# Attention of block 1: values stationary, probabilities moving, and the gate applied to the transposed output

## The chip, the cores and the metric

The kernel runs on one core of a Trainium2 chip. The metric is device time in microseconds (us) of one execution of the whole program, median of several runs. TensorE (PE) multiplies matrices and does the transposes; VectorE (DVE), ScalarE (ACT) and GpSimd (POOL) work on tiles; SyncE (SP) issues most DMAs. In the rows, PEld is the loading of the stationary operand, which runs beside PE.

## The reference

Everything is float32; `x` is (1, 256, 2048): 256 tokens. The program is two layers of a gated convolution beside windowed attention (block 1), then an RWKV and a latent-attention mixer with a feed-forward part (block 2, which the change does not touch). What matters of block 1, in one layer:

```python
u = hn @ w_in[i]
a_val, a_glu, a_z, q, k, v, b_z = jnp.split(u, offs, axis=-1)
ya = _conformer_conv(a_val, a_glu, ...) * jax.nn.silu(a_z)
# attention: 16 query heads of 64, in 4 groups with one key and value head each
s = q·k * 64**-0.5 + bias_band            # window of 128 on both sides
m = maximum(max(s), sink);  e = exp(s - m)
denom = sum(e) + exp(sink - m)
yb = ((e / denom) @ v) * jax.nn.silu(b_z)
h = h + concatenate([ya, yb]) @ w_out[i]
```

With 256 tokens and blocks of 128 every query sees both blocks of keys, so a head's probabilities are a 256x256 matrix with the band in the bias.

## The kernel before, in words

**Projections.** The hidden state lies in memory with channels on the 128 partitions and 256 tokens along the free axis. A projection to 256 columns (`lin`) splits weights and activations into a high and a low half and adds three matmuls (L302, L303, L304) for each of 16 slices of channels and each of two output tiles: 96 matmuls. Weights come by DMA as `wraw`, in blocks of four slices (24 matmuls); ACT casts the high half (`whi`, L264) and DVE subtracts for the low half (`wlo`, L265), with three buffers of each. The sum stands in one of three PSUM buffers "lin".

**A layer.** `layer1` first projects the convolution's eight inputs, then keys and values, then goes through four attention steps j = 0 to 3. A step projects q (tile `q`, L478) and the gate `gz` = silu(b_z) with tokens on partitions (L490), calls `attend1` for four heads, and then has the 31 convolution steps of two channel tiles on ACT and DVE (`cy`, L501), which need nothing of the attention. Behind the loop follow the sum over channels (`cs`, L507), the four `z` projections, whose result DVE takes out of PSUM (L408), and `w_out`, attention half first.

**attend1 before.** For each of the four heads g: scores by four matmuls (L588), then bias, sink and maximum in one DVE reduction for each half (L593), into a tile of the ring "s", which has four buffers and also serves the `z` tiles. Then the sink's term `ex` (L596, L598), eight exponentials on ACT with their sums (L601), the sum and its reciprocal `den` on DVE (L603, L604). For each head four PE transposes of the probabilities into `ptr` (L611), a copy to `pT` on ACT (L613), and four matmuls `po` (L616) in which a 128x128 piece of `pT` is stationary and 64 columns of values `vd` move: the output has tokens on partitions. It is scaled by `den` (L619), multiplied by `gz` (L621), transposed by four PE transposes `pot` (L625) and split into `Y` (L626).

**Buffers and order.** The tiles `q`, `pT` and the outputs of the convolution come from rings with few buffers: tag "q" has two, tag "pT" two. In PSUM `ptr`, `pot` share two buffers, `sc` has two and `po` one. Each engine works through its instructions in a fixed order, made when the program is built: a scheduler merges the strands (attention, projections, weight loads and splits, convolution) by their readiness in its own model and by priorities, and within one engine nothing overtakes. PE fills the gaps of the attention with projection matmuls in this way.

Of the kernel before, what the change touches and what calls it, by code (L numbers as in the profile page):

```python
# [8 lines left out]
F32 = mybir.dt.float32  # L9
# [3 lines left out]
ALU = mybir.AluOpType  # L13
# [5 lines left out]
SEQ = 256  # L19
# [78 lines left out]
class Kern:  # L98
# [475 lines left out]
    def attend1(self, i, j, q, vd, gz, Y):  # L574
        nc = self.nc
        sk = self.sink[i][:, 4 * j : 4 * j + 4]
        mx = self.wk.tile([128, 4, 2], F32, tag="mx", name=self.nm("mx"))
        den = self.wk.tile([128, 4, 2], F32, tag="den", name=self.nm("den"))
        ex = self.wk.tile([128, 4, 2], F32, tag="ex", name=self.nm("ex"))
        s4 = []  # L580
        for g in range(4):
            h = 4 * j + g
            bt = self.wk.tile([128, 384], F32, tag="bt", name=self.nm("bt"))
            nc.gpsimd.dma_start(bt[:], self.bias_src(h))
            ps = self.psum("sc", [128, 2, SEQ], "sc")
            for qb in range(2):
                for u in range(2):
                    nc.tensor.matmul(ps[:, qb, :], lhsT=q[:, g, qb * 128 : qb * 128 + 128], rhs=self.ks[u][:, j, :],  # L588
                                     start=(u == 0), stop=(u == 1))
            s = self.wk.tile([128, 2, SEQ], F32, tag="s", bufs=4, name=self.nm("s"))  # L590
            for qb in range(2):
                o = 128 * (1 - qb)
                nc.vector.tensor_tensor_reduce(s[:, qb, :], ps[:, qb, :], bt[:, o : o + SEQ], 1.0, sk[:, g : g + 1],  # L593
                                               ALU.add, ALU.max, mx[:, g, qb : qb + 1])
            s4.append(s)
        nc.vector.tensor_tensor(ex[:], sk.unsqueeze(2).to_broadcast([128, 4, 2]), mx[:], ALU.subtract)  # L596
        nc.vector.tensor_scalar(mx[:], mx[:], -1.0, None, ALU.mult)
        nc.scalar.activation(ex[:], ex[:], AF.Exp)  # L598
        for g in range(4):
            for qb in range(2):  # L600
                nc.scalar.activation(s4[g][:, qb, :], s4[g][:, qb, :], AF.Exp, bias=mx[:, g, qb : qb + 1],  # L601
                                     accum_out=den[:, g, qb : qb + 1])
        nc.vector.tensor_tensor(den[:], den[:], ex[:], ALU.add)  # L603
        nc.vector.reciprocal(den[:], den[:])  # L604
        po = self.psum("o", [128, 2, 4, 64], "po")
        for g in range(4):
            s = s4[g]
            pt = self.psum("tr", [128, 2, SEQ], "ptr")
            for kb in range(2):
                for qb in range(2):  # L610
                    nc.tensor.transpose(pt[:, kb, qb * 128 : qb * 128 + 128], s[:, qb, kb * 128 : kb * 128 + 128], self.ident)  # L611
            pT = self.wk.tile([128, 2, SEQ], F32, tag="pT", name=self.nm("pT"))
            nc.scalar.copy(pT[:], pt[:])  # L613
            for qb in range(2):
                for kb in range(2):
                    nc.tensor.matmul(po[:, qb, g, :], lhsT=pT[:, kb, qb * 128 : qb * 128 + 128], rhs=vd[:, kb, j, :],  # L616
                                     start=(kb == 0), stop=(kb == 1))
        on = self.wk.tile([128, 2, 4, 64], F32, tag="pT", name=self.nm("on"))
        nc.vector.tensor_tensor(on[:], po[:], den[:].rearrange("p g b -> p b g").unsqueeze(3).to_broadcast([128, 2, 4, 64]), ALU.mult)  # L619
        on_ = on[:].rearrange("p b g c -> p b (g c)")  # L620
        nc.vector.tensor_tensor(on_, on_, gz[:], ALU.mult)  # L621
        pt = self.psum("tr", [128, 2, SEQ], "pot")
        for t in range(2):
            for qb in range(2):
                nc.tensor.transpose(pt[:, t, qb * 128 : qb * 128 + 128],  # L625
                                    on[:, qb, 2 * t : 2 * t + 2, :].rearrange("p g c -> p (g c)"), self.ident)  # L626
        self.split_pair(Y, 8 + 2 * j, pt[:])

    def embed_new(self, i):

# [851 lines left out]
```

## Time and profile before

| | |
|---|---|
| time, median of 3 runs | 2235.72 us (2234.7 to 2237.15) |
| profiled execution | 2232.6 us |
| its span, first to last instruction | 2230.7 us |
| PE busy | 2203.2 us, 99% |
| DVE busy | 1638.7 us, 73% |
| ACT busy | 1157.5 us, 52% |
| attention steps of layer 0 / layer 1 | about 140 to 290 us / 730 to 870 us |

Busy time is time in which an engine has at least one instruction running. Matmuls overlap in PE's pipeline, so that one of them lasts 0.28 us while the next starts 0.12 us later; what a matmul costs is read from start to start. An fp32 matmul is recorded as several passes, and the count behind the x counts passes.

### The profile page before, as it was taken

Reading aid. Unit: us, or ns where it says so; the run is one execution under the profiler, and the core shown is the slowest. Engines: PE = TensorE matmul, PEld = TensorE weight load, DVE = VectorE, ACT = ScalarE, POOL = GpSimd, SP = SyncE. Lnnn points to the kernel's source line nnn. Section 1 sums busy time; section 2 is a strip of 40 time slices with the busy share of each in tenths; the row PEclk is TensorE's granted clock in tenths of the full one; section 3 lists DMA queues with packets and bytes.
Section 4 is the critical chain, followed back from the end, with each engine's and each line's share of the span. In section 5 each row is a group of like instructions: output and inputs, shape, how many; then the busy total and the mean of one; then the engine's idle time right before and its main releaser. Section 6 shows DMA issues by size and latency. Waiting matters only on the chain.

```text
span 2230.7 us, 43513 instructions
## 1 busy us (share of the span) xinstructions
PE 2203.2 (99%) x17563; PEld 2134.6 (96%) x17563; DVE 1638.7 (73%) x2884; ACT 1157.5 (52%) x1694; POOL 106.6 (5%) x253
## 2 busy tenths in 40 slices
PE   8999999999999999999999999999999999999998
PEld 8999999999999999999999889999998999899987
DVE  6999988677999887677878886676665566556665
ACT  6456646454467555556656665355443444434443
POOL 3100000000000000002100000010000000000000
PEclk9999999999999999999999999999999999999999
DMA  7875557666665466667675434477655666556654
GB/s 239 241 208 158 158 180 214 187 204 183 184 185 161 143 196 212 212 202 230 197 189 142 130 118 136 147 233 226 182 188 191 187 183 187 189 189 185 184 189 142
DMA packets 382745, 413.23 MB, mean 185 GB/s; under 512 B 40472, under 2 KB 343829, under 8 KB 382160
## 3 DMA queue, kind: packets, MB, share of 16 engines
q1 hardware_dynamic: 344672, 366.06, 53.4%
q0 software_dynamic: 10960, 31.79, 4.5%
q10 hardware_dynamic: 26912, 12.60, 2.5%
q8 instruction: 138, 2.26, 0.4%
q14 instruction: 63, 0.52, 0.1%
HBM read 390.47 MB, written 19.92 MB: 184 GB/s over the span
## 4 chain that ended last, share of the span: by engine, by line
PE 96%; DVE 2%; ACT 1%; issue 0%; DMA 0%; ACTq 0%; SPq 0%; DVEq 0%
PE lin L302 25%; PE lin L304 25%; PE lin L303 25%; PE lin L1299 2%; PE lin L1300 2%; PE lin L1298 2%; PE dn L1300 2%; PE dn L1299 2%; PE dn L1298 2%; PE po L616 1%; PE sc L588 1%; PE lin L1136 1%; PE lin L1134 1%; PE lin L1135 1%; PE ptr L611 1%; PE pch L1017 1%
## 5 line engine op out<-in xcount | busy, mean ns | idle before, releaser
L264 ACT CAST whi<-wraw 128x1024 fp32r<-128x1024 f32 (+1 forms) x709 | 725.4, 1024 | 914.5 <-PE lin L303 632.4
L302 PE MATMUL lin<-xh,whi 128*128 128x256 f32 x4080 | 1158.8, 284 | 2.3 <-ACT ev L656 1.2
L304 PE MATMUL lin<-xh,wlo 128*128 128x256 f32 x4080 | 1157.7, 284 | 0.6 <-DVE wlo L265 0.6
L303 PE MATMUL lin<-xl,whi 128*128 128x256 f32 x4080 | 1157.4, 284 | 0.0
L265 DVE TENSOR_TENSOR wlo<-wraw,whi 128x1024 fp32r<-128x1024 f32 (+1 forms) x709 | 844.5, 1192 | 408.1 <-ACT whi L264 404.8
L302 PEld LDWEIGHTS lin<-xh,whi 128*128 128x128 f32 x4080 | 782.7, 192 | 5.5 <-issue 1.9
L304 PEld LDWEIGHTS lin<-xh,wlo 128*128 128x128 f32 x4080 | 782.7, 192 | 2.2 <-issue 1.0
L303 PEld LDWEIGHTS lin<-xl,whi 128*128 128x128 f32 x4080 | 782.7, 192 | 1.4 <-issue 1.0
L501 DVE SCALAR_TENSOR_TENSOR cy<-apad,vc_cw,cy 128x256 f32<-128x256 f32 x480 | 229.9, 481 | 7.8
L304 PE MATMUL lin<-whi,xl 128*128 128x256 f32 x320 | 91.7, 287 | 0.0
L302 PE MATMUL lin<-whi,xh 128*128 128x256 f32 x320 | 91.6, 286 | 0.0
L303 PE MATMUL lin<-wlo,xh 128*128 128x256 f32 x320 | 90.8, 284 | 0.0
L304 PE MATMUL lin<-yh,wlo 128*128 128x256 f32 x256 | 73.4, 288 | 0.8 <-DVE wlo L265 0.7
L302 PE MATMUL lin<-yh,whi 128*128 128x256 f32 x256 | 73.0, 286 | 0.2 <-ACT mla L1208 0.2
L303 PE MATMUL lin<-yl,whi 128*128 128x256 f32 x256 | 73.1, 286 | 0.0
L1299 PE MATMUL lin<-wlo,xh 128*128 128x512 f32 (+1 forms) x176 | 67.1, 381 | 0.5 <-DVE wlo L265 0.5
L1298 PE MATMUL lin<-whi,xh 128*128 128x512 f32 (+1 forms) x176 | 67.1, 381 | 0.4 <-ACT whi L264 0.4
L1298 PE MATMUL dn<-whi,xh 128*128 128x512 f32 (+1 forms) x176 | 67.0, 381 | 0.0
L1299 PE MATMUL dn<-wlo,xh 128*128 128x512 f32 (+1 forms) x176 | 67.0, 381 | 0.0
L1300 PE MATMUL lin<-whi,xl 128*128 128x512 f32 (+1 forms) x176 | 67.0, 381 | 0.0
L1300 PE MATMUL dn<-whi,xl 128*128 128x512 f32 (+1 forms) x176 | 67.0, 381 | 0.0
L302 PEld LDWEIGHTS lin<-whi,xh 128*128 128x128 f32 x320 | 61.3, 192 | 0.0
(533 smaller groups left out, 2505.5 us busy)
## 6 DMA issues: line engine op xcount, KB each, us to landing
wraw<-in_w_in_dram SPq DMA_DIRECT2D x244, 512.0 KB, 3.8
wraw<-in_w_out_dram SPq DMA_DIRECT2D x88, 512.0 KB, 3.8
wraw<-in_ffn_w_gate_dram SPq DMA_DIRECT2D x88, 512.0 KB, 3.6
wraw<-in_ffn_w_up_dram SPq DMA_DIRECT2D x88, 512.0 KB, 3.5
wraw<-in_ffn_w_down_dram SPq DMA_DIRECT2D x87, 512.0 KB, 3.7
wraw<-in_w_pg_dram SPq DMA_DIRECT2D x64, 512.0 KB, 4.5
bt<-btab POOLq DMA_DIRECT2D x32, 192.0 KB, 3.3
btab<-bF ACTq DMA_DIRECT2D x4, 1024.0 KB, 7.9
```

The costliest lines, as they stand in the source:

```text
L264: nc.scalar.copy(hi[:], src)
L265: self.lo = nc.vector.tensor_tensor(lo[:], src, hi[:].bitcast(F32), ALU.subtract)
L302: nc.tensor.matmul(ps[:, t, :], lhsT=h, rhs=xh_, start=((t, k) == first), stop=False)
L303: nc.tensor.matmul(ps[:, t, :], lhsT=h, rhs=xl_, start=False, stop=False)
L304: nc.tensor.matmul(ps[:, t, :], lhsT=l, rhs=xh_, start=False, stop=((t, k) == last))
L501: prev, tail = tail, nc.vector.scalar_tensor_tensor(y, ap[:, t, k : k + SEQ], cw[:, k : k + 1], y, ALU.mult, ALU.add)
L588: nc.tensor.matmul(ps[:, qb, :], lhsT=q[:, g, qb * 128 : qb * 128 + 128], rhs=self.ks[u][:, j, :], start=(u == 0), stop=(u == 1))
L611: nc.tensor.transpose(pt[:, kb, qb * 128 : qb * 128 + 128], s[:, qb, kb * 128 : kb * 128 + 128], self.ident)
L616: nc.tensor.matmul(po[:, qb, g, :], lhsT=pT[:, kb, qb * 128 : qb * 128 + 128], rhs=vd[:, kb, j, :], start=(kb == 0), stop=(kb == 1))
L1298: nc.tensor.matmul(ps, lhsT=zh, rhs=hi, start=(k == 0), stop=False)
L1299: nc.tensor.matmul(ps, lhsT=zh, rhs=lo, start=False, stop=False)
L1300: nc.tensor.matmul(ps, lhsT=zl, rhs=hi, start=False, stop=(k == nt - 1))
```

## The change

The product with the values is turned round. The values (64 columns) are stationary and 256 columns of `pT` move, so the output comes out with channels on partitions, as `Y` needs it: head 2t on partitions 0 to 63, head 2t+1 on partitions 64 to 127 of one tile. The gate and the softmax sum, which lie with tokens on partitions, are multiplied first (`gn`), transposed in place of the output (`pgt`, four transposes) and copied to `gT` by ACT; the output `y` is `po` times `gT`. `gT` and `y` take buffers of the tag "q".

```diff
@@ -602,29 +602,37 @@
                                      accum_out=den[:, g, qb : qb + 1])
         nc.vector.tensor_tensor(den[:], den[:], ex[:], ALU.add)
         nc.vector.reciprocal(den[:], den[:])
-        po = self.psum("o", [128, 2, 4, 64], "po")
-        for g in range(4):
-            s = s4[g]
-            pt = self.psum("tr", [128, 2, SEQ], "ptr")
-            for kb in range(2):
-                for qb in range(2):
-                    nc.tensor.transpose(pt[:, kb, qb * 128 : qb * 128 + 128], s[:, qb, kb * 128 : kb * 128 + 128], self.ident)
-            pT = self.wk.tile([128, 2, SEQ], F32, tag="pT", name=self.nm("pT"))
-            nc.scalar.copy(pT[:], pt[:])
-            for qb in range(2):
-                for kb in range(2):
-                    nc.tensor.matmul(po[:, qb, g, :], lhsT=pT[:, kb, qb * 128 : qb * 128 + 128], rhs=vd[:, kb, j, :],
-                                     start=(kb == 0), stop=(kb == 1))
-        on = self.wk.tile([128, 2, 4, 64], F32, tag="pT", name=self.nm("on"))
-        nc.vector.tensor_tensor(on[:], po[:], den[:].rearrange("p g b -> p b g").unsqueeze(3).to_broadcast([128, 2, 4, 64]), ALU.mult)
-        on_ = on[:].rearrange("p b g c -> p b (g c)")
-        nc.vector.tensor_tensor(on_, on_, gz[:], ALU.mult)
-        pt = self.psum("tr", [128, 2, SEQ], "pot")
+
+        gn = self.wk.tile([128, 2, 4, 64], F32, tag="pT", name=self.nm("gn"))
+        nc.vector.tensor_tensor(gn[:], gz[:].rearrange("p b (g c) -> p b g c", g=4),
+                                den[:].rearrange("p g b -> p b g").unsqueeze(3).to_broadcast([128, 2, 4, 64]), ALU.mult)
+        pt = self.psum("tr", [128, 2, SEQ], "pgt")
         for t in range(2):
             for qb in range(2):
                 nc.tensor.transpose(pt[:, t, qb * 128 : qb * 128 + 128],
-                                    on[:, qb, 2 * t : 2 * t + 2, :].rearrange("p g c -> p (g c)"), self.ident)
-        self.split_pair(Y, 8 + 2 * j, pt[:])
+                                    gn[:, qb, 2 * t : 2 * t + 2, :].rearrange("p g c -> p (g c)"), self.ident)
+        gT = self.wk.tile([128, 2, SEQ], F32, tag="q", name=self.nm("gT"))
+        nc.scalar.copy(gT[:], pt[:])
+
+        po = self.psum("o", [128, 2, SEQ], "po")
+        for t in range(2):
+            pTs = []
+            for h in range(2):
+                s = s4[2 * t + h]
+                pt = self.psum("tr", [128, 2, SEQ], "ptr")
+                for kb in range(2):
+                    for qb in range(2):
+                        nc.tensor.transpose(pt[:, kb, qb * 128 : qb * 128 + 128], s[:, qb, kb * 128 : kb * 128 + 128], self.ident)
+                pT = self.wk.tile([128, 2, SEQ], F32, tag="pT", name=self.nm("pT"))
+                nc.scalar.copy(pT[:], pt[:])
+                pTs.append(pT)
+            for kb in range(2):
+                for h in range(2):
+                    nc.tensor.matmul(po[64 * h : 64 * h + 64, t, :], lhsT=vd[:, kb, j, :], rhs=pTs[h][:, kb, :],
+                                     start=(t == 0 and kb == 0), stop=(t == 1 and kb == 1))
+        y = self.wk.tile([128, 2, SEQ], F32, tag="q", name=self.nm("ya"))
+        nc.vector.tensor_tensor(y[:], po[:], gT[:], ALU.mult)
+        self.split_pair(Y, 8 + 2 * j, y[:])
 
     def embed_new(self, i):
 
```

The order on PE in the last step (j = 3) of layer 0. `sc` are the last scores, `ptr` the transposes of the probabilities, `lin` with `xh`, `xl` projections. Before, from the first transposes of the step:

```order
L302 MATMUL lin_3450<-xh_88,whi_3459 128x256
L611 MATMUL ptr_3153<-cblk,s_3106 128x128
L303 MATMUL lin_3450<-xl_90,whi_3459 128x256
L304 MATMUL lin_3450<-xh_88,wlo_3460 128x256
L302 MATMUL lin_3450<-xh_88,whi_3459 128x256
L611 MATMUL ptr_3153<-cblk,s_3106 128x128 x3
```

The same place now:

```order
L588 MATMUL sc_3116<-kh,qs_2950 128x256
L588 MATMUL sc_3116<-kl,qs_2950 128x256
L303 MATMUL lin_3560<-xl_91,whi_3653 128x256
L304 MATMUL lin_3560<-xh_89,wlo_3654 128x256
L612 MATMUL pgt_3139<-cblk,gn_3137 128x128 x4
L625 MATMUL ptr_3147<-cblk,s_3091 128x128 x4
L625 MATMUL ptr_3154<-cblk,s_3101 128x128 x4
L631 MATMUL po_3146<-pT_3152,vd_1542 64x256
L625 MATMUL ptr_3165<-cblk,s_3111 128x128 x4
L302 MATMUL lin_3690<-xh_88,whi_3699 128x256
```

Before, the first transposes stand among the matmuls of a projection; now two projection matmuls stand between the last scores and the transposes of the gate, and those stand ahead of every transpose of the probabilities.

The order on DVE in the same step, around the softmax sum `den`; `cy` are convolution steps, `z` takes a `z` projection out of PSUM. Before:

```order
L501 SCALAR_TENSOR_TENSOR cy_261<-apad_1282,vc_cw_643,cy_261 128x256 x2
L408 TENSOR_TENSOR z_3441<-lin_3320,r_224 128x512
L501 SCALAR_TENSOR_TENSOR cy_261<-apad_1282,vc_cw_643,cy_261 128x256
L603 TENSOR_TENSOR den_3097<-den_3097,ex_3098 128x8
L501 SCALAR_TENSOR_TENSOR cy_261<-apad_1282,vc_cw_643,cy_261 128x256
L604 RECIPROCAL den_3097<-den_3097 128x8
L265 TENSOR_TENSOR wlo_3516<-wraw_3455,whi_3515 128x1024
```

And now:

```order
L501 SCALAR_TENSOR_TENSOR cy_261<-apad_1282,vc_cw_643,cy_261 128x256 x8
L603 TENSOR_TENSOR den_3082<-den_3082,ex_3083 128x8
L501 SCALAR_TENSOR_TENSOR cy_261<-apad_1282,vc_cw_643,cy_261 128x256
L604 RECIPROCAL den_3082<-den_3082 128x8
L501 SCALAR_TENSOR_TENSOR cy_261<-apad_1282,vc_cw_643,cy_261 128x256
L607 TENSOR_TENSOR gn_3137<-gz_3078,den_3082 128x512
L501 SCALAR_TENSOR_TENSOR cy_261<-apad_1282,vc_cw_643,cy_261 128x256 x5
L408 TENSOR_TENSOR z_3421<-lin_3300,r_224 128x512
```

The gate's product `gn` follows the reciprocal with one convolution step between, and the first `z` comes behind it instead of ahead of the sum.

The order on PE in step j = 2 of layer 1, the last three heads' values matmuls; `ppt` is a transpose of the embedding's part. Before, the last head:

```order
L303 MATMUL lin_8896<-wlo_8990,xh_5103 128x256
L304 MATMUL lin_8896<-whi_8989,xl_5105 128x256
L616 MATMUL po_8637<-vd_7466,pT_8665 128x64 x4
L616 MATMUL po_8637<-vd_7466,pT_8676 128x64 x4
L302 MATMUL lin_8896<-whi_8989,xh_5103 128x256
```

And now:

```order
L631 MATMUL po_8616<-pT_8622,vd_7446 64x256
L625 MATMUL ptr_8635<-cblk,s_8581 128x128 x4
L631 MATMUL po_8616<-pT_8629,vd_7446 64x256
L631 MATMUL po_8616<-pT_8622,vd_7446 64x256
L631 MATMUL po_8616<-pT_8629,vd_7446 64x256
L625 MATMUL ptr_8642<-cblk,s_8591 128x128 x4
L631 MATMUL po_8616<-pT_8640,vd_7446 64x256
L645 MATMUL ppt_8659<-cblk,pr_8657 128x128 x4
L631 MATMUL po_8616<-pT_8647,vd_7446 64x256
L631 MATMUL po_8616<-pT_8640,vd_7446 64x256
L631 MATMUL po_8616<-pT_8647,vd_7446 64x256
L302 MATMUL lin_9464<-xh_5082,whi_9473 128x256
```

Each pair of heads has one values matmul alone and then three together; before, the last run stands within a projection, now the next projection starts behind it.

## Rows read from the trace of the kernel before

**Rows 1.** The page: busy time of each engine with its share of the span, and the chain of work that ended last by engine.

```profile
PE 2203.2 (99%) x17563; PEld 2134.6 (96%) x17563; DVE 1638.7 (73%) x2884; ACT 1157.5 (52%) x1694; POOL 106.6 (5%) x253
...
PE 96%; DVE 2%; ACT 1%; issue 0%; DMA 0%; ACTq 0%; SPq 0%; DVEq 0%
```

**Rows 2.** The list of PE's waits, its first rows: what waited, for what, us in total, times, longest.

```profile
PE vps L170 <- DMA cblk<-in_c_blk_dram: 2.9, 1, 2.9
PE xt L356 <- DMA xr<-in_x_dram: 2.7, 1, 2.7
```

**Rows 3.** The timeline of PE at a values matmul of layer 0: start and duration in us, what.

```profile
175.23 0.28 PE L303 MATMUL lin<-wlo,xh 128*128 128x256 f32 x1
175.35 1.00 PE L616 MATMUL po<-vd,pT 128*128 128x64 f32 x8
...
176.37 0.28 PE L302 MATMUL lin<-whi,xh 128*128 128x256 f32 x1
```

**Rows 4.** The timeline of PE at the sum over channels, fp32 over 256 columns, and at the transposes of the output behind it.

```profile
275.89 2.32 PE L507 MATMUL cs<-cy,cblk 128*128 128x256 f32 x10
278.05 0.60 PE L625 MATMUL pot<-cblk,on 128*128 128x128 f32 x4
278.49 0.60 PE L507 MATMUL cs<-cy,cblk 128*128 128x256 f32 x2
```

**Rows 5.** The timeline of PE in block 2: a run of matmuls of which `pch` use 64 columns of the array and `po` 64 rows and 64 columns, between projection matmuls (rows and columns used stand behind the names, as 128\*64).

```profile
1183.83 0.28 PE L303 MATMUL lin<-xl,whi 128*128 128x256 f32 x1
1184.03 0.68 PE L1030 MATMUL pch<-big 128*64 128x64 f32 x8
1184.64 0.67 PE L1033 MATMUL po<-big,tx 64*64 64x64 f32 x8
...
1185.47 0.28 PE L302 MATMUL lin<-xh,whi 128*128 128x256 f32 x1
```

**Rows 6.** The timeline of PE in block 2: a run on 64 rows of the array, between projection matmuls.

```profile
1102.17 0.28 PE L302 MATMUL lin<-xh,whi 128*128 128x256 f32 x1
1102.38 1.13 PE L848 MATMUL pw<-hwz,la 64*128 64x256 f32 x4
...
1103.66 0.28 PE L304 MATMUL lin<-xh,wlo 128*128 128x256 f32 x1
```

**Rows 7.** The timeline of PE in block 2: two such matmuls of four passes each, `pw` on one half of the array's rows and `pa` on the other; the first pair and the last of four.

```profile
1023.23 0.48 PE L848 MATMUL pw<-hwz,la 64*128 64x256 f32 x1
1023.24 0.48 PE L854 MATMUL pa<-hwz,la 64*128 64x256 f32 x1
...
1023.99 0.38 PE L854 MATMUL pa<-hwz,la 64*128 64x256 f32 x1
```

**Rows 8.** Two answers on single lines. L408 (DVE takes `z` out of PSUM): what its idle time before it ended with, us and times. L584 (the bias row's load by POOL's queue): time from issue to landing.

```profile
  PE ptr L611: 1.6, 2
...
DMA to landing us min/median/max: 2.6/3.3/6.0
```

**Rows 9.** The timelines of PE, DVE and ACT in the last step of layer 0, from the last scores to the reciprocal of the softmax sum; in square brackets the idle time before and what ended it.

```profile
252.44 0.28 PE L588 MATMUL sc<-kl,qs 128*128 128x256 f32 x1
...
253.34 0.48 DVE L593 CUSTOM_DVE_ANT_0 s<-sc,bt,sink 128x256 f32<-128x256 f32 x1
...
254.15 0.48 DVE L501 SCALAR_TENSOR_TENSOR cy<-apad,vc_cw,cy 128x256 f32<-128x256 f32 x1
...
256.16 0.16 DVE L597 TENSOR_SCALAR mx<-mx 128x8 f32<-128x8 f32 x1
...
261.30 0.69 DVE L408 TENSOR_TENSOR z<-lin,r 128x512 f32<-128x512 f32 x1 [0.93 <-PE ptr L611]
...
262.78 0.17 DVE L603 TENSOR_TENSOR den<-den,ex 128x8 f32<-128x8 f32 x1 [0.40 <-ACT s L601]
...
263.26 0.20 DVE L604 RECIPROCAL den<-den 128x8 f32<-128x8 f32 x1
...
256.23 1.05 ACT L264 CAST whi<-wraw 128x1024 fp32r<-128x1024 f32 x1 [1.83 <-DVE cy L501]
...
258.59 0.21 ACT L598 ACTIVATE ex<-ex 128x8 f32<-128x8 f32 x1
258.71 0.49 ACT L601 ACTIVATE s<-s,mx 128x256 f32<-128x256 f32 x1
```

**Rows 10.** Groups by line: line, engine, operation, shape, passes or instructions | busy us, mean ns of one | idle time of the engine just before, and what ended it.

```profile
L611 PE MATMUL ptr<-cblk,s 128*128 128x128 f32 x128 | 21.2, 273 | 0.0
...
L613 ACT COPY pT<-ptr 128x512 f32<-128x512 f32 x32 | 17.7, 584 | 6.3 <-PE ptr L611 6.2
```

**Rows 11.** Windows (us, then busy time with instructions of PE, PEld, DVE, ACT, POOL, the granted clock as a share of full speed, DMA share, GB/s): the attention of layer 0, and two at the end of the program. Then the timeline of PE at the start of the program.

```profile
140.00:290.00 150.00, 150.00 (x1264) 149.52 (x1264) 135.81 (x278) 94.46 (x165) 9.76 (x21) 1.00 0.56 167
2221.00:2222.00 1.00, 0.24 (x3) 0.04 (x1) 0.42 (x1) 0.41 (x2) 0.00 (x0) 1.00 0.53 207
...
2225.00:2226.00 1.00, 0.00 (x0) 0.00 (x0) 0.92 (x3) 1.00 (x2) 0.00 (x0) 0.50 0.00 0
...
8.49 0.58 PE L302 MATMUL lin<-xh,whi 128*128 128x256 f32 x1 [0.65 <-ACT whi L264]
...
12.63 0.41 PE L303 MATMUL lin<-xl,whi 128*128 128x256 f32 x1
12.84 0.32 PE L304 MATMUL lin<-xh,wlo 128*128 128x256 f32 x1
```

## The prediction

> **What bounds the kernel now.** I read the page first, then TensorE's list of waits, then timelines around the attention of block 1, and only then the order of the instructions. The page has TensorE (PE) busy for 99% of the span and puts 96% of the chain that ended last on it [rows 1]. The list of waits says the same from the other side: its longest entries are the first two loads, and nothing in the attention makes PE wait for more than a microsecond [rows 2]. So whatever PE has to do more, or any wait put in front of it, is paid in full; work on VectorE (DVE, 73%) and ScalarE (ACT, 52%) is paid only where PE comes to wait for it. The profiled execution took 2232.6 us, 3.1 below the median of 2235.72; I sum against the former and add 3.1 at the end.
>
> **The values matmul itself.** The attention step runs 8 times (2 layers, 4 groups of heads). Before, each step has 16 fp32 matmuls of 64 columns, which the trace records as 32 passes. A run of 8 passes between projection matmuls costs 0.90: from 175.23 to 176.37 is 1.14, less two projection matmuls at 0.12 [rows 3]. Four such runs are 3.6 us a step. The transposes of the probabilities (16) and of the output or gate (4) are as many after as before: no difference.
>
> After, a step has 8 matmuls of 256 columns, 16 passes. Of an fp32 pass over 256 columns the trace shows 0.216 (ten of them from 275.89 to 278.05) [rows 4]. If the two column halves run one after the other, that is 16 x 0.216 = 3.5, no gain at all; the gain must come from halves that run side by side. The new order breaks each tile's four matmuls into one alone (first half, 2 passes) and three together (second, first, second half, 6 passes), with projection or transposes between. The lone one takes 0.43 either way; the three take 0.86 if the halves overlap, 1.29 if not.
>
> To this comes the change of the array's shape. A run on 64 columns (128\*64) and then on 64\*64 costs 1.64 from matmul to matmul, of which 16 passes at 0.058 and two projection matmuls explain 1.17: 0.47 for three changes, about 0.33 for going in and out [rows 5]. A run on 64 rows gives 0.39: 1.49 less 0.24 less 4 x 0.216 [rows 6]. I take 0.33, the row with the column shape. Each step has four such runs: 2 x (0.43 + 0.33) + 2 x (0.86 + 0.33) = 3.90 with overlap, 4.76 without, against 3.6. Over 8 steps: +2.4 or +9.3 us; with free changes of shape and full overlap, -8.2.
>
> Which? No row shows two column halves at once. The nearest row is of two row halves: pw and pa start 0.01 apart, four times, and the four pairs take the time of four passes [rows 7]. I take overlap, +2.4. [...]
>
> **The wait before the last step of each layer.** This is the larger part. The gate over the softmax sum (gn) is needed before anything else of the step: its four transposes (pgt) now stand ahead of the probabilities' transposes in PE's order. So PE waits for all eight exponentials, the sum, the reciprocal and gn, where before a head's transpose waited for its own exponentials alone. In steps 0 to 2 the order has 88 to 120 projection matmuls between the last scores and pgt, 10.6 us or more at 0.12, which covers the chain. In the last step it has 2 in layer 0 and 29 in layer 1: q and y of the step now share one ring of two buffers, so q of step j+1 waits for y of step j, the scores come about a projection later, and by then the three "lin" PSUM buffers hold z projections. These wait in turn for score buffers of the last step, as z waits for ptr already now [rows 8]. The next projection cannot start.
>
> The chain, from the start S of the last scores matmul, by starts of layer 0 before [rows 9] in the new order's sequence: matmul 0.28, two score reductions 0.81, then conv step, weight split, ex and conv step 2.01 (254.15 to 256.16), negation 0.16: 3.26. Eight exponentials up to the sum's start 4.07 (258.71 to 262.78): 7.33. Sum to reciprocal 0.48, reciprocal and a conv step 0.50, gn 0.69 (taken as z's 128x512 row): S + 9.0. PE is through with its two matmuls at S + 0.36: **8.6 idle in layer 0**. In layer 1 the reductions of the last two heads follow each other closely, and a cast (whi) stands ahead of ex on ACT whose buffer comes free when PE ends its 29 matmuls, at S + 3.6; cast 1.05, ex 0.2, 4.07, 1.67 make S + 10.6: **7.0 idle**. Taken whole instead, the row of before is 10.34 from last scores to sum (252.44 to 262.78) [rows 9], with 1.67 then 11.6 and 8.4 idle. That is one bound; the other leaves out splits and conv steps: 6.1 and 2.9. I take 8.6 and 7.0, since the casts' places are known. A late bias row (landing 3.3 median, up to 6.0) [rows 8] can add up to 2.7.
>
> Smaller waits. After pgt the second probabilities' transpose needs the PSUM buffer that ACT copies out (gT), then po needs the copy of the first: 0.60 + 0.58 + 0.58 against 12 transposes at 0.11 [rows 4, 10], about 0.5 in each last step: 1.0. In layer 1, step 2, nothing of the projection is left behind the last po, and z2 waits for y, for q and for what stands between on DVE: 0.38 + 0.61 + 0.61 + 0.40 + 0.69, less PE's own 0.22 = 2.5. Sum of idle time 8.6 + 7.0 + 1.0 + 2.5 = 19.1.
>
> **The clock.** The granted clock reads 1.00 in 2221:2222, with PE's last three matmuls, and 0.50 in 2225:2226, with PE idle between [rows 11]. [...] At the start PE's matmuls still stand 0.21 apart at 12.84, against the 0.12 above; taken as the slow pace, from 8.49 it lasted 4.3 us, in which 1.9 were lost. Of that I count 1.4 for each of the two gaps, since 0.5 falls into the waits behind pgt: 2.8; at least 0, at most 3.8. [...]
>
> **What costs nothing.** DVE has three 128x512 passes a step before and after (gn, y and the low half in place of two scalings and the low half). ACT gets one copy more, 0.58 x 8, on an engine half idle; where it is on the path I counted it. SP's queue (weights) keeps its order and POOL only swaps two memsets, so bias and weight loads are asked for as before. From the second half of layer 1's output projection on, PE's order is the same to the end. Where the weight splits are late the three-buffer rings hold two blocks of 24 matmuls, 5.8 us; if that cover goes, each late split costs up to 1.14.
>
> **Sum.** 19.1 + 2.8 + 2.4 = 24.3; 2232.6 + 24.3 + 3.1 = 2260.0 us.
>
> **Rivals.** (a) The halves run one after the other: 9.3 in place of 2.4, 2266.9. For it: no row has two column halves at once. Against it: rows 7.
> (b) The chain is as long as the row of before, with a late bias: 11.6 + 8.4 + 1.0 + 2.5 + 3.8 + 2.4 = 29.7, and up to 2.7 more: 2265 to 2268. For it: DVE is busy for 135.8 of 150 us in this stretch of layer 0 [rows 11]. Against it: before, ACT loads a table and a cast ahead of the exponentials there (256.23 to 258.71) [rows 9], which the new order does not have in the last step of layer 0.
> (c) PE does not stand idle, because the chain hides behind something that I did not see: +2.4, 2238.1, within what can be told from no change. For it: not one transpose of the probabilities waited before [rows 10]. Against it: PE takes its instructions in order, and 2 or 29 matmuls are 0.24 or 3.5 us of a chain of nine.
> (d) It is faster: the halves overlap, the change of shape is hidden behind the loads of the next weights, and the scores of the last step come early enough. Then only -8.2 is left, 2227.5. It decides where the idle time in both last steps together is under 4 us.
>
> **How the numbers follow.** Forecast 0.55, (a) 0.17, (b) 0.16, (c) 0.08, (d) 0.04. A difference under 0.2% (4.5 us) cannot be told from none in this kernel. Slower: forecast, (a) and (b), 0.88; within it (c), 0.08; faster (d), 0.04. The forecast's own range is 2254 to 2266. The range to hold 8 in 10 goes down to both chains at their shorter bound (12.5 idle, no clock, 2.4: 2250.6) and up to the longer ones with halves in turn (29.7 + 6.9 + 2.7: 2275): 2249 to 2276.
>
> **What would show it.** In the profile after: PE waiting for gn (at pgt) about 8.6 us near 255 to 265 and 7.0 near 750, the only long waits that are new; a wait of z's first projection for q of some 2.5 us in layer 1; a granted clock under 1.00 behind the two long ones; po passes of the two halves at pairwise equal starts, 0.216 from pair to pair, and some 0.1 lost at each end of a run. PE's busy time should change by little. It is wrong if pgt waits for less than 3 us in both last steps, or if PE's idle time grows by 15 us and the total does not.

## The result, and the profile after

The changed kernel took 2262.54 us (median of 4 runs, 2260.07 to 2263.28) against 2236.06 for the kernel before: 26.5 us more, ratio 1.0114 with a 95% interval of 1.0101 to 1.0126. The forecast was 2260.0.

The page of the changed kernel, engines, as [rows 1]:

```profile
span 2261.5 us, 43254 instructions
PE 2215.5 (98%) x17435; PEld 2126.1 (94%) x17435; DVE 1640.7 (73%) x2884; ACT 1157.4 (51%) x1698; POOL 106.7 (5%) x253
```

The list of PE's waits, as [rows 2] (us in total, times, longest):

```profile
PE pgt L612 <- DVE gn L607: 17.3, 2, 9.5
...
PE lin L302 <- DVE q L478: 2.4, 1, 2.4
```

These are the two new waits for gn and the new wait for q, 19.7 us of standing still. The place in layer 0, timelines of PE and DVE, as [rows 9]:

```profile
282.61 0.28 PE L588 MATMUL sc<-kl,qs 128*128 128x256 f32 x1
...
282.85 0.28 PE L304 MATMUL lin<-xh,wlo 128*128 128x256 f32 x1
292.67 1.08 PE L612 MATMUL pgt<-cblk,gn 128*128 128x128 f32 x4 [9.54 <-DVE gn L607]
293.55 2.00 PE L625 MATMUL ptr<-cblk,s 128*128 128x128 f32 x8
295.48 0.90 PE L631 MATMUL po<-pT,vd 128*64 128x256 f32 x2
...
282.87 0.48 DVE L501 SCALAR_TENSOR_TENSOR cy<-apad,vc_cw,cy 128x256 f32<-128x256 f32 x1
283.75 0.48 DVE L593 CUSTOM_DVE_ANT_0 s<-sc,bt,sink 128x256 f32<-128x256 f32 x1 [0.41 <-DMA bt<-btab]
...
290.84 0.17 DVE L603 TENSOR_TENSOR den<-den,ex 128x8 f32<-128x8 f32 x1
...
291.84 0.68 DVE L607 TENSOR_TENSOR gn<-gz,den 128x512 f32<-128x512 f32 x1
```

The windows behind it (columns as in [rows 11], the granted clock third from the end):

```profile
292.00:293.00 1.00, 0.33 (x2) 0.36 (x3) 0.96 (x3) 0.00 (x0) 0.00 (x0) 0.50 0.00 0
...
295.00:296.00 1.00, 1.00 (x5) 0.44 (x3) 1.00 (x3) 0.65 (x2) 0.00 (x0) 0.50 0.00 0
296.00:297.00 1.00, 1.00 (x8) 0.69 (x7) 0.96 (x3) 0.98 (x2) 0.00 (x0) 0.99 0.07 16
```

PE has done its two projection matmuls and waits for the whole chain on DVE and ACT. When it goes on, the granted clock stands at 0.50 until about 296 (0.99 in 296:297): eight transposes take 1.93 us (293.55 to 295.48), 0.24 each, against 0.11 in [rows 4].

The two forms of the values matmul in the changed kernel, timeline of PE, as [rows 3]:

```profile
182.14 0.65 PE L631 MATMUL po<-pT,vd 128*64 128x256 f32 x2
182.72 0.38 PE L304 MATMUL lin<-whi,xl 128*128 128x256 f32 x1
182.94 0.28 PE L302 MATMUL lin<-whi,xh 128*128 128x256 f32 x1
...
259.61 0.28 PE L302 MATMUL lin<-xh,whi 128*128 128x256 f32 x1
259.82 1.08 PE L631 MATMUL po<-pT,vd 128*64 128x256 f32 x6
260.83 0.66 PE L625 MATMUL ptr<-cblk,s 128*128 128x128 f32 x4
```

Six passes of 0.216 in turn would be 1.30; they take 1.01 from start to start (259.82 to 260.83). The lone matmul has two passes and takes 0.58 (182.14 to 182.72).

Where the 26.5 went can be read from the first `pc` matmul (the sum of a norm) behind each layer; timelines of PE, layer 0 and layer 1 before, then after:

```profile
514.35 0.39 PE L208 MATMUL pc<-cblk,acc 128*128 128x1 f32 x3
...
999.00 0.28 PE L208 MATMUL pc<-cblk,acc 128*128 128x1 f32 x2
...
524.12 0.50 PE L208 MATMUL pc<-cblk,acc 128*128 128x1 f32 x4
...
1023.93 0.28 PE L208 MATMUL pc<-cblk,acc 128*128 128x1 f32 x2
```

So layer 0 lost 9.8 us and layer 1 15.2, 24.9 together. In block 2, whose order on PE is the same, this profile is 5.9 us longer than that of before; but the profiles of all twelve experiments have it 2 to 7 us longer too, those of before_short_conv and before_q_on_pool among them (about 4.3 each), whose times are not above that of before. So I take it that the one profile of before has a short block 2, and that the 24.9 are the change's; the 1.6 that are left of the 26.5 lie within the spread of the single runs.

### The profile page after: what moved, and what is told of

The parts are those of the page before. It is cut to its first block, busy times and chain, and to the rows that moved or that the text cites. A ratio compares the mean times of both kernels' runs of the same rounds, so it can differ in the third digit from the quotient of the medians.

```text
span 2261.5 us, 43254 instructions
## 1 busy us (share of the span) xinstructions
PE 2215.5 (98%) x17435; PEld 2126.1 (94%) x17435; DVE 1640.7 (73%) x2884; ACT 1157.4 (51%) x1698; POOL 106.7 (5%) x253
## 4 chain that ended last, share of the span: by engine, by line
PE 92%; DVE 3%; issue 2%; ACT 1%; DMA 1%; ACTq 0%; SPq 0%; POOL 0%; DVEq 0%; POOLq 0%
PE lin L304 24%; PE lin L303 24%; PE lin L302 24%; PE lin L1307 2%; PE lin L1308 2%; PE lin L1306 2%; PE dn L1308 2%; PE dn L1307 2%; PE dn L1306 2%; PE po L631 1%; DVE wlo L265 1%; PE ptr L625 1%; PE lin L1144 1%; PE lin L1142 1%; PE lin L1143 1%
## 5 line engine op out<-in xcount | busy, mean ns | idle before, releaser
L304 PEld LDWEIGHTS lin<-whi,xl 128*128 128x128 f32 x320 | 61.4, 192 | 1.5 <-issue 1.5
```

Source lines behind the costliest of these rows:

```text
L304: nc.tensor.matmul(ps[:, t, :], lhsT=l, rhs=xh_, start=False, stop=((t, k) == last))
```

## The experiments

What stood to be told apart: does the loss come from the shared ring, which makes the last scores late, from the place of the gate's transposes, or from the matmuls themselves; and could a form of the change gain time?

**Own buffers for gT and y.**

```diff
-        gT = self.wk.tile([128, 2, SEQ], F32, tag="q", name=self.nm("gT"))
+        gT = self.w1.tile([128, 2, SEQ], F32, tag="sg", name=self.nm("gT"))
...
-        y = self.wk.tile([128, 2, SEQ], F32, tag="q", name=self.nm("ya"))
+        y = self.w1.tile([128, 2, SEQ], F32, tag="sq", name=self.nm("ya"))
```

> The changed kernel with gT and y in two buffers that are free at that time (those of sg and sq) in place of the ring of q. Theory (the shared ring holds up q of the next step, so the last scores come late and little is left to cover the chain to gn): the order now has 102 and 150 projection matmuls between the last scores and pgt, 12 and 18 us against a chain of about 10. Both waits at pgt go (19.7 us of PE waits with that for q), and with them the three slow stretches (5.4). Left is the values matmul, 3.9 against 3.6 a step: 2236.1 + 2.6 = 2239, within 2236 to 2242. Rival (the wait comes from pgt standing ahead of every ptr, whatever the ring): waits of 4 us and more remain at pgt in every last step, 2250 or above.

Measured 2257.29 us, ratio to before 1.0097 (1.0084 to 1.0110). Both expectations failed: pgt waits no longer, but 18 of the expected 23 us came back elsewhere. PE's waits:

```profile
PE pc L208 <- DVE lnacc L205: 8.2, 2, 4.9
```

Timelines of PE and DVE in layer 0:

```profile
341.26 0.95 PE L208 MATMUL pc<-cblk,lnacc 128*128 128x1 f32 x4 [4.86 <-DVE lnacc L205]
...
330.71 0.48 DVE L501 SCALAR_TENSOR_TENSOR cy<-apad,vc_cw,cy 128x256 f32<-128x256 f32 x1
```

A window behind it:

```profile
343.00:345.00 2.00, 2.00 (x11) 2.00 (x10) 1.80 (x7) 0.97 (x3) 0.54 (x1) 0.50 0.48 182
```

PE now waits for the LayerNorm sum, which DVE makes from the convolution, and the clock falls there instead, to 0.50 in 343:345: 28 matmuls take 6.1 us (342.08 to 348.18) where 3.4 would do at 0.12 each, as ahead of the wait. The last convolution step starts at 330.71. In the kernel before it ended at 320.08:

```profile
319.08 1.00 DVE L501 SCALAR_TENSOR_TENSOR cy<-apad,vc_cw,cy 128x256 f32<-128x256 f32 x2
```

So DVE is late behind PE. In the changed kernel it caught up while PE stood at pgt: there the convolution of layer 0 ends at 318.75. In own_ring DVE itself stands idle more: 21.0 of the 170 us from 140 to 310, against 16.1 before. The list of DVE's waits names the scores, which come from PE, own_ring first, then before:

```profile
DVE s L593 <- PE sc L588: 5.6, 4, 1.7
...
DVE s L593 <- PE sc L588: 0.4, 1, 0.4
```

These 5 us are about half of the 11 by which the convolution ends later; where the other half comes from was not followed up.

**The first z in its own buffer.** In `layer1`, z of j = 0 takes the buffer of sg (`silu_pair` is told where to take it from):

```diff
-            zz = self.silu_pair(pz, r2, "s", 4)
+            zz = self.silu_pair(pz, r2, "s", 4) if j else self.silu_pair(pz, r2, "sg", 1, self.w1)
```

> The changed kernel, with the first z projection's tile in the buffer of sg instead of the ring that it shares with the scores; gT and y stay in the ring of q. Theory: the last scores stay late, but in layer 0 PE can go on with z (102 projection matmuls ahead of pgt instead of 2), so the wait of 9.5 us and its slow stretch go (11.2), in layer 1 pgt has 20 instead of 29 and waits about 8.8 (1.1 more), and z2's wait for q goes with its slow stretch (4.1): 2262.5 - 11.2 - 4.1 + 1.1 = 2248, within 2244 to 2252. Rival (the score ring has no part in it, PE would wait for gn anyway): within 2 us of 2262.5.

Measured 2257.03 (1.0099, 1.0086 to 1.0112). The wait for gn in layer 0 went, that in layer 1 stayed (8.3), as expected; but 4.9 us of waiting for the LayerNorm sum came up in layer 0. Places right, time wrong by 9.

**The gate behind the products.** The lines from gn to gT stand behind the loop over t, ahead of y:

```diff
         nc.vector.reciprocal(den[:], den[:])
-        gn = self.wk.tile([128, 2, 4, 64], F32, tag="pT", name=self.nm("gn"))
...
-        nc.scalar.copy(gT[:], pt[:])
         po = self.psum("o", [128, 2, SEQ], "po")
...
+        gn = self.wk.tile([128, 2, 4, 64], F32, tag="pT", name=self.nm("gn"))
...
+        nc.scalar.copy(gT[:], pt[:])
         y = self.wk.tile([128, 2, SEQ], F32, tag="q", name=self.nm("ya"))
```

> The changed kernel, with gn, pgt and gT written behind the four heads' products instead of ahead of them; the ring of q stays shared. Theory: the scores stay late, but a probabilities' transpose waits for its own exponentials alone, as before the change; in the last steps ptr stands behind 1 projection matmul (layer 0) and none (layer 1), so PE still waits there for the first head: 3.3 + 1.0 + some 0.9 for the bias, about 5 in layer 0 and 5 to 6 in layer 1, together about 10.5 in place of 17.3; the wait for q (2.4) goes: 2262.5 - 6.8 - 4.1 = 2252, within 2247 to 2256. Rival (the place of pgt alone makes the wait): no wait above 2 us is left, 2240. Other rival (the place of pgt has no part): within 2 us of 2262.5.

Measured 2253.3 (1.0081, 1.0069 to 1.0093), as the theory said. PE's waits:

```profile
PE ptr L614 <- ACT s L601: 9.4, 2, 5.3
```

The first transposes now wait for their own exponentials. So with the scores late, the place of pgt makes nearly half of the wait (9.4 are left of 17.3). With the scores early, as in own_ring, it makes none: the late scores are the condition of the whole wait.

**Four together.** Own buffers, and the second head first:

```diff
             for kb in range(2):
-                for h in range(2):
+                for h in (1, 0):
                     nc.tensor.matmul(po[64 * h : 64 * h + 64, t, :], lhsT=vd[:, kb, j, :], rhs=pTs[h][:, kb, :],
```

> As own_ring, and the second head of each pair multiplied first, so that no values matmul can start until both copies are there and the four stand together in PE's order. Theory (a change of the array's shape costs 0.34 for in and out, and a lone half uses half the array): a pair takes 4 x 0.216 + 0.34 = 1.20 in place of 0.77 + 1.20, 0.77 less; 16 pairs: 12.3 less than own_ring, about 2227, and so faster than the kernel before by 9 us. Rival (the price is not in the breaks, or the wait for the second copy eats it): within 3 us of own_ring.

Measured 2243.24 (1.0033, 1.0021 to 1.0046): 14.1 less than own_ring, where 12.3 were expected; but not 2227, since own_ring itself missed. PE's timeline:

```profile
215.13 0.28 PE L303 MATMUL lin<-xl,whi 128*128 128x256 f32 x1
215.34 1.08 PE L631 MATMUL po<-pT,vd 128*64 128x256 f32 x8
216.36 0.39 PE L304 MATMUL lin<-xh,wlo 128*128 128x256 f32 x1
```

Eight passes take 1.02, as long as six did in the changed kernel: the two halves of the array's columns do run side by side. In turn, eight would be 1.73.

**DVE's load.** The last eight of the 30 convolution steps left out, in three kernels:

```diff
-                for k in range(1, 31):
+                for k in range(1, 23):
```

> The kernel before with 22 of the 30 convolution steps on DVE (the last eight taps are left out), 25.6 us of DVE less in each layer: the base for the two runs beside it. Its PE has few waits in block 1 as it is (3.7 us, most behind the sum over channels): about 2231 by either theory.

> The changed kernel with the same eight steps left out. The ring of q is shared, so the scores of the last step still come late: 29 projection matmuls ahead of pgt in both layers, waits of about 6.3 and 7.8 us, 3.7 for the slow stretches behind them, 2.6 for the values matmuls: 20.4 over before_short_conv, about 2251. If DVE's load were all that matters in the changed kernel too, it would come within 5 us of before_short_conv.

> own_ring with the same eight steps left out. own_ring had no wait at pgt, but 8.2 us of new waits at pc for the LayerNorm sum and slow stretches behind them. Theory (DVE is a second bound: its convolution ends late, and the wait that goes at pgt comes back where PE needs the convolution): with 25.6 us less on DVE in each layer this wait goes, and only the values matmuls are left: 2.6 over before_short_conv, about 2234. Rival (own_ring loses its time on PE itself or by the order of its scores, not by DVE's load): it stays some 20 us over before_short_conv, about 2251.

Measured on the same chip: 2233.06, 2251.43 and 2236.13. With less work on DVE own_ring is 3.1 over its base (2.6 expected) instead of 22.6, and has no wait at pc. The changed kernel stays 18.4 over its base, so DVE's load is not all that matters there. The parts are not those expected: the waits at pgt are 8.8 together, where 14.1 were expected and 17.3 stood with all the steps. About half of the wait thus went with DVE's load and the order made for it (29 projection matmuls ahead of pgt in layer 0 instead of 2), and half stayed with the late scores. With 2.7 for the matmuls that leaves some 7 of the 18.4 that were not taken apart, part of them slow stretches behind the waits. PE's wait in this kernel:

```profile
PE pgt L612 <- DVE gn L607: 8.8, 2, 4.5
```

So there are two bounds in a row: the late scores, and behind them the convolution on DVE.

**Gate late, own buffers, four together.** The edits of gate_late, own_ring and own_ring_four_together in one kernel.

> Three edits of the changed kernel at once: gate behind the products (gate_late), own buffers for gT and y, four values matmuls together. The order on PE is then that of the kernel before but for the runs of values matmuls (scores of the next step ahead of the gate's transposes, 75 to 80 projection matmuls between the last scores and ptr), and DVE has its pieces where before had its scalings. Theory: no new wait, 1.20 for each pair of heads against 1.80 before, 16 pairs: 9.6 less than before, 2226; faster. Rival (DVE is late in this form too, as in own_ring_four_together): 2240 to 2245.

Measured 2240.31 (1.0018, 1.0009 to 1.0027): the rival. PE's waits for the LayerNorm sum (3.8) and for ACT's piece `ev` of the embedding (4.0) come up, 6.2 of the 7.8 in layer 0. With the eight steps left out there too:

> late_own_ring_four with the last eight convolution taps left out, as in before_short_conv. It had waits of 10.0 us in layer 0 (3.7 before), at places where PE needs what DVE and ACT make of the convolution and the embedding. Theory (four values matmuls together save 0.6 a pair on PE, and DVE's late convolution took it back): without DVE's load the saving stays: before_short_conv - 9.6 = 2223.5, within 2221 to 2227. Rival (the saving is given back by something else than DVE's load): 2230 or above.

Measured 2225.01, ratio to before 0.9954 (0.9940 to 0.9967), where before_short_conv had 0.9987: 7.4 us less by the ratios, 9.6 expected, and within the theory's range. The saving on PE is real, and with all the convolution on DVE it is lost again.

**Work from DVE to POOL.** First gn alone, then gn and the low halves of y and q, on late_own_ring_four; the control changes only the last line, in the kernel before (`split_pair` is given the engine as an argument):

```diff
-        nc.vector.tensor_tensor(gn[:], gz[:].rearrange("p b (g c) -> p b g c", g=4),
+        nc.gpsimd.tensor_tensor(gn[:], gz[:].rearrange("p b (g c) -> p b g c", g=4),
...
-        self.split_pair(Y, 8 + 2 * j, y[:])
+        self.split_pair(Y, 8 + 2 * j, y[:], nc.gpsimd)
...
-                nc.vector.tensor_tensor(half(q, h), half(q, h), half(qv, h)[:, h].bitcast(F32), ALU.subtract)
+                nc.gpsimd.tensor_tensor(half(q, h), half(q, h), half(qv, h)[:, h].bitcast(F32), ALU.subtract)
```

> late_own_ring_four with gn on POOL, which is idle for most of the stretch, in place of DVE: 4 x 0.6 = 2.4 us of DVE less in each layer. Theory (in layer 0 the end of the convolution on DVE decides): layer 0 gains about 2.4 and its slow stretch a little, layer 1, which has little wait left, nothing: 2237 to 2238. Rival (POOL is slower, stands behind its bias loads or holds up DVE): 2240 or above.

> late_own_ring_four with three pieces of each step on POOL in place of DVE: gn, the low half of y and the low half of q (two of 64 partitions): 4 x (0.6 + 0.6 + 1.2) = 9.6 us of DVE less in each layer. Theory (DVE's convolution is what took the saving back): most of the saving of the values matmuls stays, 2229 to 2233, faster than before. Rival (POOL at 1.24 for such a piece makes q and the scores late, or stands behind its bias loads): 2238 or above.

> The kernel before with the low half of q on POOL instead of DVE, the piece of late_own_ring_four_three_on_pool that exists there too: the control for that run. Theory (its gain of 7.6 comes from the values matmuls standing four together, POOL only keeps DVE from taking it back): before had 3.7 us of waits in layer 0 besides the start's, so at most some 3 are gained: 2232 to 2236. Rival (the gain comes from POOL's part alone): 2228 or below.

Measured 2238.88 for gn alone (1.0020, 1.0011 to 1.0029): by the ratio no gain. With three pieces 2227.64, ratio 0.9963 (0.9950 to 0.9975): faster than both kernels, and it computes the whole reference. The control, the kernel before with its q on POOL, gained nothing: 2235.13 (1.0001, 0.9992 to 1.0010), although its convolution of layer 0 ends at 312.4 instead of 320.1. So q on POOL alone is not the gain; the other two pieces have no counterpart in the kernel before, and each was not tried by itself there. In the kernel with three pieces the convolution of layer 0 ends at 308.3, and PE has no wait for the LayerNorm sum. The timeline of DVE:

```profile
307.30 1.01 DVE L501 SCALAR_TENSOR_TENSOR cy<-apad,vc_cw,cy 128x256 f32<-128x256 f32 x2
```

DVE's longest waits from 140 to 310 us are those for casts, with three pieces on POOL first, then in late_own_ring_four:

```profile
DVE wlo L265 <- ACT whi L264: 1.8, 4, 1.2
```

```profile
DVE wlo L265 <- ACT whi L264: 7.0, 16, 1.0
```

In these 170 us DVE was busy for 163.0 with three pieces on POOL, against 153.5 without. So DVE was done earlier because it waited less, more than because it had less to do. Why the order made for this kernel spares it these waits stays open.

## Why the prediction was right

- **What bounds.** PE at 99% and nothing hiding in front of it: right, as far as the changed kernel goes. What the prediction did not see is a second bound close behind. It put DVE at "costs nothing"; own_ring and own_ring_short_conv show that DVE decides as soon as the waits at pgt are gone.
- **The values matmul.** Forecast +2.4 with overlap. From the rows above a lone matmul adds 0.58 + 0.10 at the next projection matmul + 0.09 ahead (0.77), three add 1.20: 3.94 a step against the 3.90 of the forecast, so 2.7 over 8 steps. The change of shape was put at 0.33, though two thirds of 0.47 are 0.31; it came out at 0.34. Rival (a), halves in turn, is out: eight passes as long as six.
- **The waits for gn.** 8.6 and 7.0 forecast, 9.5 and 7.8 measured. The mis-sized part of layer 0 is the start of the chain: the last head's reduction started at 283.75, 0.86 after its scores were through (282.61 + 0.28). Of this a convolution step ahead of it on DVE (282.87) makes nearly half, and the bias row the rest: DVE was idle for 0.41 until it landed. The prediction had the bias as an addition "up to 2.7" and left it out of the sum; the step it did not have. In layer 1 it was not ACT's cast that decided, as forecast. Timelines of DVE and ACT:

```profile
785.71 1.22 DVE L265 TENSOR_TENSOR wlo<-wraw,whi 128x1024 fp32r<-128x1024 f32 x1
786.85 0.16 DVE L596 TENSOR_TENSOR ex<-sink,mx 128x8 f32<-128x8 f32 x1
...
787.52 0.51 ACT L601 ACTIVATE s<-s,mx 128x256 f32<-128x256 f32 x1 [0.27 <-DVE mx L597]
```

A weight split stands ahead of `ex` on DVE, and the exponentials start 5.6 after the last scores (781.91) in place of 4.85.
- **The smaller waits** behind pgt, 1.0 in the sum, do not show as waits: PE runs there at a granted clock of 0.50 (293:296).
- **The places.** The waits were forecast near 255 to 265 and near 750 and came at 283 to 293 and 786 to 793: q is late in each step, and the delays add up. In layer 0 the last scores start 30 us later than before (252.44 in [rows 9]), not one projection later. This moved the waits; their size came out near the forecast.
- **The wait for q** in layer 1: 2.5 forecast, 2.4 measured.
- **The clock.** 2.8 forecast, about 5.3 measured. That a wait brings the clock down, for 1.4 lost each time, was the author's estimate, and no run shows the 1.4. The changed kernel shows a granted clock of 1.00 in 283:284, when PE comes to stand, of 0.50 in 286:296, and of 0.50 in 771:773 behind the wait of 2.4 for q. Two of the stretches cost 1.7 and 2.1 in place of 1.4; the third, behind the wait for q, was not counted at all. The pace was read rightly: at a granted clock of 0.50 the matmuls stand 0.21 apart here too. PE's timeline there, then windows:

```profile
770.60 0.58 PE L302 MATMUL lin<-xh,whi 128*128 128x256 f32 x1 [2.38 <-DVE q L478]
...
773.75 0.35 PE L304 MATMUL lin<-xh,wlo 128*128 128x256 f32 x1
773.94 0.28 PE L302 MATMUL lin<-xh,whi 128*128 128x256 f32 x1
```

```profile
772.00:773.00 1.00, 1.00 (x7) 1.00 (x6) 0.97 (x3) 0.62 (x1) 0.00 (x0) 0.50 0.00 0
...
774.00:775.00 1.00, 1.00 (x10) 1.00 (x10) 0.93 (x3) 0.00 (x0) 0.00 (x0) 1.00 0.00 0
```

Fifteen starts in 3.34 us (770.60 to 773.94), 1.8 at 0.12 each: 1.5 lost behind a wait of only 2.4.
- **A gain that was not in the sum.** Before, PE had waits of together 2.1 us behind the convolution of layer 0; its waits from 300 to 345:

```profile
PE lin L302 <- ACT ev L656: 1.2, 1, 1.2
PE pc L208 <- DVE lnacc L205: 0.5, 1, 0.5
PE lin L302 <- DVE hT L534: 0.4, 1, 0.4
```

They are gone after the change, because DVE catches up during the wait at pgt. Waits 19.7, clock 5.3 and matmuls 2.7 make 27.7; less 2.1 that is 25.6, against 24.9 read from the layers' ends. The forecast's own sum was 24.3. That it came so near is in part luck: the clock was 2.5 too low, and this gain of 2.1, which it did not have, made up for most of that.
- **Rivals.** (c), no standing still, is out by the 19.7. (b), the chain of before taken whole, is out: 8.2 from the last scores to the sum (282.61 to 290.84), not 10.3. (d), faster if the waits go, is out: the halves overlap, but the change of shape is not hidden (0.34 in each run of values matmuls), and own_ring had no wait at pgt and was still 22.6 slower. A faster kernel took the four matmuls together and DVE's convolution out of the way.

## What to carry to other kernels

When a new tile takes a buffer from a ring, list who allocates next from it: here it is the next step's q, and with it the scores and all that follows in the step came late. Where two engines are loaded to nine tenths in a stretch (in the kernel before PE was busy for 170.0 and DVE for 153.9 of the 170 us from 140 to 310), a wait taken from one can come up behind the other, as here (own_ring: 17.3 us at pgt gone, 8.2 at pc new); leave out part of the second one's work in a test kernel before building on the gain. And when half the array is used, let the matmuls of both halves stand together: here one alone and three together cost 0.77 more for each pair of heads than four together, and the new product saves only 0.6 even with four together.

## What the runs showed of the hardware beyond the forecast

With pieces of the work on POOL, instructions of DVE beside them lasted longer. In late_own_ring_four_three_on_pool, a weight split on DVE that meets a subtraction on POOL (timelines of DVE and POOL):

```profile
188.28 2.18 DVE L265 TENSOR_TENSOR wlo<-wraw,whi 128x1024 fp32r<-128x1024 f32 x1
...
188.05 1.31 POOL L251 TENSOR_TENSOR xl<-ya,xh 128x512 fp32r<-128x512 f32 x1
```

It took 2.18 instead of the 1.22 of a split beside an idle POOL (785.71 in the changed kernel), and all convolution steps together 249.9 instead of the 229.9 us of late_own_ring_four:

```profile
L501 DVE SCALAR_TENSOR_TENSOR cy<-apad,vc_cw,cy 128x256 f32<-128x256 f32 x480 | 249.9, 523 | 8.3
```

So the pieces on POOL gave DVE back about as much time as they took from it: its busy time is 1643.5 us, against 1638.8 in late_own_ring_four. The kernel before with q on POOL shows the same: 241.1 us for the convolution steps, against 229.9 in the kernel before. From the end of POOL's subtraction (188.05 + 1.31 = 189.36) to the end of the split (190.46) it is 1.10, near the 1.22 of a whole split; by what means the one lengthens the other, no run shows.
